# The even layer of a two-layer encoder with its tokens in parity order, and its first two value products side by side

## The chip, the core and the metric

The kernel runs on one core of a Trainium2 chip. The core has five engines that run at the same time, each with its own queue that is worked off in order: TensorE (PE) multiplies matrices, VectorE (DVE) and ScalarE (ACT) work element by element, GpSimd (POOL) and SyncE (SP) mostly start DMA transfers here. The engines wait for each other through semaphores. The metric is the device time of one execution in microseconds; 2482.04 us is the median of three runs before the change.

## The reference

The input is x with 256 tokens of 2048 numbers. Layer 0 is an even layer, layer 1 an odd one; each is a mixer with a residual, then a gated feed-forward network with a residual. What the change touches is the mixer of layer 0:

```python
y = rmsnorm(h, ln_mix[layer])
proj = einsum("bsd,de->bse", y, w_in)
# A: eight heads, three groups (window, dilation) = (128, 1), (512, 4), (2048, 16)
logits = q . k * scale + t5_bias(offset); p = softmax; o = p @ v     # per group, lse kept
out_a  = sum over groups of softmax(lse) * o
# B: four heads, two maps each
w = softmax(q1 . k1 + bias) - lam * softmax(q2 . k2 + bias);  o = rmsnorm(w @ v)
mix = concat(out_a, out_b) @ w_out
```

Groups 1 and 2 of A have dilations 4 and 16, so a query sees only keys whose distance is even. The bias of a pair depends on the bucket of key position minus query position.

## The kernel before, in words

All of the work is built around products of a 2048 by N weight with the activations of 256 tokens. Both sides are kept as two numbers in float32r, a high part and the remainder, and a product is three matmuls: high by high, high by low, low by high. Every weight unit of 512 KB is fetched by SP into `raw` (5 buffers), rounded by ACT into `wh` (L196) and subtracted by DVE into `wl` (L197). `wh` and `wl` have 4 buffers each. So the cast of unit n writes over unit n-4 and waits until PE has read that one for the last time.

There are two kinds of product. `gemm_b` (L129, L132) has weights as the stationary operand and gives queries and keys. `gemm_a` (L157 to L159) has the activations stationary and the weights moving, 512 columns at a time, and gives the values V and the output projections: 8 units, 12 matmuls each, 96 per product. Its result takes two PSUM buffers of the tag `gm`, of which there are four.

The even layer needs six V products in A, three per half of the heads (groups 0, 1, 2). Those of groups 1 and 2 need the tokens with the even ones first; `strided` reads every other column of the stationary activations (L154). The layer's norm is put in late: the products run on x times the gain (`yT`, from a transposed copy `xT`), and the factor per token `rstd` multiplies the result when V leaves PSUM (`v_tiles`, ACT L200 and DVE L203). `rstd` comes from eight squares of x on ACT (L226, two for each quarter of x), a sum (L245), a square root on ACT (L210, behind a load of its table) and a reciprocal (L212). `row_broadcast` lays it along the columns: two copies (L253), two PE transposes (L254), a copy into R (L256). Two more transposes (L403) and a copy (L404) give `rstd_par`, the factor in parity order.

At the start nine matmuls on zeros run on PE (L371). Then comes the product of group 0, whose units are taken in turn with pieces of `xT`, then two small matmuls in float32 that make the tables of biases (L410, L415), then the product of group 1, then `v_tiles` of group 0 and the rest. The tables go by DMA from POOL to DRAM (`rel`, `rel2`) and come back per head in a skewed form. The tile `vals`, from which `rel` is written, and the scratch of the squares share one buffer of the tag `junk`.

The order in which an engine's instructions stand is set by a scheduler that works on the written program; instructions that are marked (`keep_in_program_order`) stay where they are. Functions given to `later` are called some products later by `tick`.

Of the kernel before, what the change touches and what calls it, by code (L numbers as in the profile page):

```python
# [25 lines left out]
F32 = mybir.dt.float32  # L27
# [5 lines left out]
P = 128  # L33
SEQ = 256
# [23 lines left out]
def trunk_kernel(ctx: ExitStack, tc, a, out):  # L58
# [46 lines left out]
    def wunit(src, parts=1):  # L105
# [36 lines left out]
    def a_unit(ps, src, u, act, nk, strided=False, parts=1):  # L142
        last = 2 * u + 2 == nk
        a_products(ps, wunit(src[u], parts), u, act, nk, strided,
                   [(t, k) for t in range(2) for k in range(2)] if last else
                   [(t, k) for k in range(2) for t in range(2)])

    def a_products(ps, w, u, act, nk, strided, order):
# [12 lines left out]
    def gemm_a(src, act, nk, strided=False, hooks={}, first=1):  # L161

        ps = [tps("gm", 4), tps("gm", 4)]
        for u in range(nk // 2):
            if u in hooks:
                hooks[u]()
            a_unit(ps, src, u, act, nk, strided, parts=1 if u else first)
# [15 lines left out]
    def halves(ps, r, order=None):  # L183
# [11 lines left out]
    def split(dst_h, dst_l, src):  # L195
        S.copy(dst_h, src)  # L196
# [51 lines left out]
    def row_broadcast(rstd):  # L248
# [7 lines left out]
        V.tensor_copy(r, ps[:, 0:SEQ])  # L256
# [63 lines left out]

    def bias_view(b, step):
# [52 lines left out]
    def x_half(u):  # L374

        xt = att.tile([P, 2, SEQ], F32, name=nm("xT"), tag=f"qk{2 + u % 4}", bufs=1)
        nc.sync.dma_start(xt.rearrange("p a b -> p (a b)"), a["xT"][u])
        for k in range(2):
            yT.append(y_tile(xt[:, k, :], ln[:, 0, :], u * 2 + k, pin=True))

    def x_rows(c):
# [5 lines left out]
    v_ps = [gemm_a(a["eva_v"][0], yT, KT, hooks={u: lambda u=u: x_half(u) for u in range(8)}, first=2)]  # L387
    table = load("t5", (32, 28), eng=nc.sync)
    onehot = load("onehot", (32, NREL), pool=tmp, tag="rx", eng=nc.sync)
    bmask = load("bmask", (28, NREL), pool=tmp, tag="ry", eng=nc.sync)  # L390
    onehot2 = load("onehot2", (32, 256), pool=tmp, tag="rx", eng=nc.sync)
    bmask2 = load("bmask2", (16, 256), pool=tmp, tag="ry", eng=nc.sync)
# [9 lines left out]
    for t in range(2):  # L402
        T.transpose(ps[:, t, 0:P], R.rearrange("p (j r) -> p r j", r=2)[:, t, :], ident)  # L403
    V.tensor_copy(rstd_par, ps[:, :, 0])  # L404

    rel = dram.tile([28, NREL + 1], F32, name="rel")
    rel2 = dram.tile([16, 256], F32, name="rel2")
    vals = tmp.tile([28, NREL + 1], F32, name="vals", tag="junk", bufs=1)
    ps = tps("s", 2)
    T.matmul(ps[0:28, 0:NREL], table, onehot, start=True, stop=True)  # L410
    V.tensor_tensor(vals[:, 0:NREL], ps[0:28, 0:NREL], bmask, op=ALU.add)
    G.dma_start(rel[:, 0:NREL], vals[:, 0:NREL])
    vals2 = tmp.tile([16, 256], F32, name="vals2", tag="rb")
    ps = tps("s", 2)
# [516 lines left out]
```

## Time and profile before

| | us |
|---|---|
| median of three runs | 2482.04 |
| the profiled execution's own time | 2482.04 |
| its span, first to last instruction | 2480.2 |
| PE busy in the span | 2469.6 |
| DVE busy | 1656.3 |
| ACT busy | 1242.2 |

The share of busy time of PE is one of a pipeline: a matmul of 512 columns is shown as 0.39 us long, but the next one starts 0.227 us after it. What one costs is read from the starts that follow each other. Times in the trace count from the start of the span; the execution's own time is 1.8 us longer than the span.

### The profile page before, as it was taken

The page shows a single profiled execution, that of the slowest core. Times are in us where ns is not written, and L with a number is a line of the kernel's source. Part 1 is how long each engine was busy: PE and PEld are TensorE (multiplying, and loading weights), DVE is VectorE, ACT ScalarE, POOL GpSimd, SP SyncE. Part 2 cuts the span into 40 slices and gives each one's busy share as a digit, 9 for nine tenths or more (in the row PEclk, how much of TensorE's full clock was granted, in tenths as well). Part 3 has the DMA queues.
Part 4 walks back from the last instruction along what each step waited for, and adds up shares of the span by engine and source line. Part 5 has one row for each costly group of instructions (what it writes and reads, how often), then busy time and mean ns, then how long its engine had stood idle before and what let it go on. Part 6 is the DMA issues. An engine that isn't in the chain of part 4 may idle for free.

```text
span 2480.2 us, 34338 instructions
## 1 busy us (share of the span) xinstructions
PE 2469.6 (100%) x13115; PEld 2125.7 (86%) x13115; DVE 1656.3 (67%) x2460; ACT 1242.2 (50%) x1859; POOL 44.2 (2%) x71
## 2 busy tenths in 40 slices
PE   9999999999999999999999999999999999999998
PEld 7888888888888888888888888888888888888887
DVE  6676567676577775477775568665777755777754
ACT  6454445465554444344444457545544443444543
POOL 0000000000000000000000000100000000000000
PEclk9999999999999999999999999999999999999999
DMA  8655566556555665566665555765566655666664
GB/s 290 194 174 178 180 182 187 173 180 180 174 187 187 188 190 195 193 188 190 191 189 193 187 184 165 174 176 178 185 190 188 192 191 194 189 192 188 188 195 144
DMA packets 130239, 463.86 MB, mean 187 GB/s; under 512 B 15248, under 2 KB 15884, under 8 KB 130074
## 3 DMA queue, kind: packets, MB, share of 16 engines
q1 hardware_dynamic: 127018, 455.05, 57.2%
q0 software_dynamic: 2624, 6.32, 2.7%
q8 instruction: 102, 1.67, 0.3%
q14 instruction: 63, 0.52, 0.1%
q10 hardware_dynamic: 432, 0.30, 0.0%
HBM read 459.44 MB, written 2.17 MB: 186 GB/s over the span
## 4 chain that ended last, share of the span: by engine, by line
PE 99%; DMA 0%; DVE 0%; ACT 0%; SPq 0%; issue 0%; DVEq 0%
PE gm L129 38%; PE gm L132 20%; PE gm L158 13%; PE gm L157 13%; PE gm L159 13%; PE tp L333 0%; PE tp L240 0%; PE s L317 0%; PE s L318 0%; PE s L316 0%; DMA raw<-in_eva_v 0%; PE s L477 0%; PE s L446 0%; PE s L345 0%; PE s L344 0%; PE s L470 0%
## 5 line engine op out<-in xcount | busy, mean ns | idle before, releaser
L197 DVE TENSOR_TENSOR wl<-raw,wh 128x1024 fp32r<-128x1024 f32 (+1 forms) x857 | 1046.4, 1222 | 414.3 <-ACT wh L196 411.1
L196 ACT CAST wh<-raw 128x1024 fp32r<-128x1024 f32 (+1 forms) x857 | 899.8, 1050 | 549.9 <-PE gm L159 422.2
L129 PE MATMUL gm<-yT,wh 128*128 128x512 f32 x4096 | 991.2, 391 | 0.0
L129 PEld LDWEIGHTS gm<-yT,wh 128*128 128x128 f32 x4096 | 748.9, 188 | 142.7
L132 PEld LDWEIGHTS gm<-yT,wl 128*128 128x128 f32 x4096 | 525.9, 191 | 21.6 <-ACT yT L200 1.2
L132 PE MATMUL gm<-yT,wl 128*128 128x256 f32 x4096 | 534.0, 283 | 0.0
L187 DVE TENSOR_TENSOR t<-t,gm 128x256 f32<-128x256 f32 x256 | 107.6, 420 | 333.7 <-ACT t L186 333.7
L186 ACT COPY t<-gm 128x256 f32<-128x256 f32 x256 | 95.4, 372 | 389.9 <-PE gm L129 389.7
L157 PE MATMUL gm<-wh,prod 128*128 128x512 f32 x704 | 274.4, 390 | 0.0
L159 PE MATMUL gm<-wh,prod 128*128 128x512 f32 x704 | 274.2, 390 | 0.0
L158 PE MATMUL gm<-wl,prod 128*128 128x512 f32 x704 | 273.9, 389 | 0.0
L158 PE MATMUL gm<-wl,yT 128*128 128x512 f32 x416 | 163.7, 394 | 0.5 <-DVE wl L197 0.5
L157 PE MATMUL gm<-wh,yT 128*128 128x512 f32 x416 | 163.9, 396 | 0.3 <-ACT wh L196 0.3
L159 PE MATMUL gm<-wh,yT 128*128 128x512 f32 x416 | 163.2, 392 | 0.0
L158 PEld LDWEIGHTS gm<-wl,prod 128*128 128x128 f32 x704 | 132.2, 188 | 27.4
L157 PEld LDWEIGHTS gm<-wh,prod 128*128 128x128 f32 x704 | 132.2, 188 | 27.2
L159 PEld LDWEIGHTS gm<-wh,prod 128*128 128x128 f32 x704 | 132.2, 188 | 27.2
L623 ACT ACTIVATE cv<-cv 128x256 f32<-128x256 f32 x88 | 36.8, 419 | 166.0 <-DVE cv L621 166.0
L157 PE MATMUL gm<-wh,mix 128*128 128x512 f32 x256 | 101.0, 395 | 0.0
L158 PE MATMUL gm<-wl,mix 128*128 128x512 f32 x256 | 100.4, 392 | 0.0
L159 PE MATMUL gm<-wh,mix 128*128 128x512 f32 x256 | 100.2, 393 | 0.0
L158 PEld LDWEIGHTS gm<-wl,yT 128*128 128x128 f32 x416 | 79.3, 191 | 17.1 <-DVE wl L197 1.4
(215 smaller groups left out, 1548.9 us busy)
## 6 DMA issues: line engine op xcount, KB each, us to landing
raw<-in_up SPq DMA_DIRECT2D x352, 512.0 KB, 3.6
raw<-in_down SPq DMA_DIRECT2D x176, 512.0 KB, 3.7
raw<-in_eva_qk SPq DMA_DIRECT2D x96, 512.0 KB, 3.4
raw<-in_eva_v SPq DMA_DIRECT2D x47, 512.0 KB, 4.0
raw<-in_evb_qk SPq DMA_DIRECT2D x32, 512.0 KB, 3.4
raw<-in_ev_out SPq DMA_DIRECT2D x32, 512.0 KB, 3.4
raw<-in_od_qk SPq DMA_DIRECT2D x32, 512.0 KB, 3.8
raw<-in_od_out SPq DMA_DIRECT2D x32, 512.0 KB, 3.4
```

What stands on the lines that cost most here:

```text
L129: T.matmul(flat, wh[:, sl], y.rearrange("p a b -> p (a b)"), start=(u == 0 and k == 0), stop=(u * 8 + k == KT - 1))
L132: T.matmul(ps[:, 1, :], wl[:, sl], y[:, 0, :], start=False, stop=False)
L157: T.matmul(ps[t], ah, wh[:, sl], start=(kt == 0), stop=False)
L158: T.matmul(ps[t], ah, wl[:, sl], start=False, stop=False)
L159: T.matmul(ps[t], al, wh[:, sl], start=False, stop=(kt == nk - 1))
L186: S.copy(t0, ps[:, 0, :])
L187: V.tensor_tensor(t0, t0, ps[:, 1, :], op=ALU.add)
L196: S.copy(dst_h, src)
L197: V.tensor_tensor(dst_l, src, dst_h.bitcast(F32), op=ALU.subtract)
L623: S.activation(c, c, AF.Gelu_apprx_tanh)
```

## The change

The transposed copy of x, from which the layer's activations are made, holds the even tokens first and then the odd ones. So all of the even layer's products have their tokens in that order, no stationary operand is read with a stride, and the reorderings that stood at single places go or move: `halves` needs no parity order, R is made in parity order, the bias is read in parity order (`parity_bias`, `by_parity`), and B's result is put back in order at its end.

The first two V products (groups 0 and 1) run side by side: for each of eight steps one piece of `xT`, one unit of the first and one of the second. All four `gm` buffers are taken by them. Their `v_tiles` all use `rstd_par`. The first unit's two halves are cast with the second activation tile in between, in a fixed order.

The tables of biases are made inside this loop, after the sixth step, by two float32r matmuls from a high and a low part of the table (`rel_tables`); the table of the even strides is every other column of the one result.

```diff
-    def wunit(src, parts=1):
+    def wunit(src, parts=1, between=None):
...
-            split(wh[:, sl], wl[:, sl], raw[:, sl])
+            split(wh[:, sl], wl[:, sl], raw[:, sl], pin=between is not None)
+            if between and i == 0:
+                between()
...
-            if strided:
-                ah, al = (act[kt][:, x, :].rearrange("p (j r) -> p r j", r=2)[:, t, :] for x in range(2))
-            else:
-                ah, al = (act[kt][:, x, t * P:(t + 1) * P] for x in range(2))
+            ah, al = (act[kt][:, x, t * P:(t + 1) * P] for x in range(2))
...
-        if order in (parity, parity_rev):
-            V.tensor_tensor(order(t2), natural(t0), natural(r), op=ALU.mult)
-        else:
-            V.tensor_tensor(order(t2) if order else t2, t0, r, op=ALU.mult)
+        V.tensor_tensor(order(t2) if order else t2, t0, r, op=ALU.mult)
...
-        V.tensor_copy(r, ps[:, 0:SEQ])
+        if by_parity:
+            V.tensor_copy(parity(r), natural(ps[:, 0:SEQ]))
+        else:
+            V.tensor_copy(r, ps[:, 0:SEQ])
...
-    v_ps = [gemm_a(a["eva_v"][0], yT, KT, hooks={u: lambda u=u: x_half(u) for u in range(8)}, first=2)]
...
-    v_ps.append(gemm_a(a["eva_v"][1], yT, KT, strided=True,
-                       hooks={u: lambda u=u: x_rows(u) for u in range(4)}))
...
+        th, tl = (tmp.tile([32, 28], F32R, name=nm("t5"), tag=f"t5{x}", bufs=1) for x in range(2))
+        split(th, tl, table)
+        oh = tmp.tile([32, NREL + 1], F32R, name="onehot_r", tag="scc")
+        S.copy(oh, onehot)
+        ps = tps("s", 2)
+        T.matmul(ps[0:28, :], th, oh, start=True, stop=False)
+        T.matmul(ps[0:28, :], tl, oh, start=False, stop=True)
+        vals = tmp.tile([28, NREL + 1], F32, name="vals", tag="junk", bufs=1)
+        V.tensor_tensor(vals, ps[0:28, :], bmask, op=ALU.add)
+        G.dma_start(rel, vals)
...
+    v_ps = [[tps("gm", 4), tps("gm", 4)] for _ in range(2)]
+    for u in range(8):
+        xt = att.tile([P, 2, SEQ], F32, name=nm("xT"), tag=f"qk{2 + u % 4}", bufs=1)
+        nc.sync.dma_start(xt.rearrange("p a b -> p (a b)"), a["xT"][u])
+        x_tile(xt, u, 0)
+        if u:
+            x_tile(xt, u, 1)
+        for g in range(2):
+            a_unit(v_ps[g], a["eva_v"][g], u, yT, KT, parts=1 if u else 2,
+                   between=None if u or g else lambda: x_tile(xt, 0, 1))
+        if u == 2:
+            rel_loads()
+        if 3 <= u < 7:
+            x_rows(u - 3)
+        if u == 5:
+            rel_tables()
+        tick()
     for c in range(4):
         squares(c)
-    rstd = row_factor()
-    R = row_broadcast(rstd)
+    R = row_broadcast(row_factor(), by_parity=True)
...
-            vg.append(v_tiles(ps, rstd_par if g else rstd, range(8 + 4 * g, 12 + 4 * g)))
+            vg.append(v_tiles(ps, rstd_par, range(8 + 4 * g, 12 + 4 * g)))
```

What this does to the order on ACT: the eight squares (`junk`, from x in `h`) and the casts of weight units (`wh`). Before, they stood in pairs among the casts of group 1's product, with the square root's table behind the last pair:

```order
L226 ACTIVATE junk_83_480,ssq_78_471<-h_75 128x512
L226 ACTIVATE junk_84_482,ssq_78_471<-h_75 128x512
L196 CAST wh_61_364<-raw_60_362 128x1024
L226 ACTIVATE junk_85_484,ssq_78_471<-h_75 128x512
L226 ACTIVATE junk_86_486,ssq_78_471<-h_75 128x512
L196 CAST wh_64_383<-raw_63_381 128x1024
L210 ACT_TABLE_LOAD
L210 ACTIVATE var_88_490<-var_88_490 128x2
```

In the changed kernel this stands at the same place; `wh_76` and `wh_79` are the last units of the two side-by-side products, `wh_110` to `wh_119` the first four units of the third one:

```order
L194 CAST wh_79_473<-raw_78_471 128x1024
L226 ACTIVATE junk_83_492,ssq_81_489<-h_75 128x512
L194 CAST wh_110_549<-raw_109_547 128x1024
L226 ACTIVATE junk_84_494,ssq_81_489<-h_75 128x512
L194 CAST wh_113_567<-raw_112_565 128x1024
L226 ACTIVATE junk_85_496,ssq_81_489<-h_75 128x512
L194 CAST wh_116_585<-raw_115_583 128x1024
L226 ACTIVATE junk_86_498,ssq_81_489<-h_75 128x512
L194 CAST wh_119_603<-raw_118_601 128x1024
L226 ACTIVATE junk_87_500,ssq_81_489<-h_75 128x512
L226 ACTIVATE junk_88_502,ssq_81_489<-h_75 128x512
L226 ACTIVATE junk_89_504,ssq_81_489<-h_75 128x512
```

The squares moved behind the casts: the first (`junk_82`) stands just ahead of `wh_79`, and the last three behind `wh_119`, which takes the buffer of `wh_79`. Behind `junk_89` follow the table load, the root and the four `v_tiles` of ACT.

On PE, the end of the product ahead of the third one, before (`tp` are the transposes of `row_broadcast` and of `rstd_par`, `gm_106` and `gm_107` the third product):

```order
L157 MATMUL gm_53_322<-wh_76_455,yT_48_290 128x512
L158 MATMUL gm_53_322<-wl_77_456,yT_48_290 128x512
L159 MATMUL gm_53_322<-wh_76_455,yT_48_290 128x512
L254 MATMUL tp_90_495<-ident_93,rb_91_496 128x128
L254 MATMUL tp_90_495<-ident_93,rb_92_499 128x128
L157 MATMUL gm_106_539<-wh_109_543,yT_5_102 128x512
L158 MATMUL gm_106_539<-wl_110_544,yT_5_102 128x512
L159 MATMUL gm_106_539<-wh_109_543,yT_5_102 128x512
L157 MATMUL gm_107_540<-wh_109_543,yT_5_102 128x512
L403 MATMUL tp_95_507<-ident_93,R_93_502 128x128 x2
```

And the same place in the changed kernel, where the third product writes `gm_107` and `gm_108`:

```order
L158 MATMUL gm_5_103<-wh_79_473,yT_74_450 128x512
L159 MATMUL gm_5_103<-wl_80_474,yT_74_450 128x512
L160 MATMUL gm_5_103<-wh_79_473,yT_74_450 128x512
L254 MATMUL tp_93_513<-ident_93,rb_94_514 128x128
L254 MATMUL tp_93_513<-ident_93,rb_95_517 128x128
L443 MATMUL tp_98_525<-ident_93,R_96_520 128x128 x2
L158 MATMUL gm_107_545<-wh_110_549,yT_7_106 128x512
```

The four transposes now stand together ahead of the third product, and that product's first matmul writes the buffer of `gm_2`, which `v_tiles` has to empty first.

## Rows read from the trace of the kernel before

**Rows 1.** The page: busy time, share of the span and count of PE and others; and the chain of work that ended last, as shares of the span by engine.

```profile
PE 2469.6 (100%) x13115; PEld 2125.7 (86%) x13115; DVE 1656.3 (67%) x2460; ACT 1242.2 (50%) x1859; POOL 44.2 (2%) x71
...
PE 99%; DMA 0%; DVE 0%; ACT 0%; SPq 0%; issue 0%; DVEq 0%
```

**Rows 2.** The timeline of PE in the first 13 us: start, length (both us), engine, line, what it writes and reads, how many in one row, and in brackets the idle time before it and who ended that.

```profile
1.49 4.21 PE L371 MATMUL s<-zeros 128*128 128x512 f32 x9 [1.49 <-DVE zeros L368]
5.49 1.06 PE L157 MATMUL gm<-wh,yT 128*128 128x512 f32 x2
...
6.71 0.40 PE L159 MATMUL gm<-wh,yT 128*128 128x512 f32 x1
...
8.63 0.39 PE L159 MATMUL gm<-wh,yT 128*128 128x512 f32 x1
9.33 0.73 PE L157 MATMUL gm<-wh,yT 128*128 128x512 f32 x2 [0.31 <-ACT wh L196]
10.59 0.50 PE L158 MATMUL gm<-wl,yT 128*128 128x512 f32 x1 [0.53 <-DVE wl L197]
```

**Rows 3.** The timeline of PE from the first product (group 0, activations read in one piece) over the two tables into the second (group 1, read with a stride). Between the first two rows' starts, 20.29 and 29.13, lie 39 matmuls, and as many between the last two's, 42.32 and 51.51.

```profile
20.29 0.39 PE L159 MATMUL gm<-wh,yT 128*128 128x512 f32 x1
...
29.13 0.39 PE L159 MATMUL gm<-wh,yT 128*128 128x512 f32 x1
29.45 1.04 PE L410 MATMUL s<-onehot,t 32*28 32x511 f32 x2
...
31.08 0.60 PE L415 MATMUL s<-onehot,t 32*16 32x256 f32 x2
31.61 0.51 PE L158 MATMUL gm<-wl,yT 128*128 128x512 f32 x1
...
42.32 0.40 PE L159 MATMUL gm<-wh,yT 128*128 128x512 f32 x1
...
51.51 0.40 PE L159 MATMUL gm<-wh,yT 128*128 128x512 f32 x1
```

**Rows 4.** The timeline of PE in the second half's product of group 1, read with a stride: between the two starts lie 51 matmuls.

```profile
257.77 0.39 PE L159 MATMUL gm<-wh,yT 128*128 128x512 f32 x1
...
269.67 0.39 PE L159 MATMUL gm<-wh,yT 128*128 128x512 f32 x1
```

**Rows 5.** The timeline of PE where the second product ends and the third begins, and where the third ends and the first product of queries begins.

```profile
53.87 0.38 PE L254 MATMUL tp<-ident,rb 128*128 128x128 f32 x2
54.00 0.48 PE L157 MATMUL gm<-wh,yT 128*128 128x512 f32 x1
...
55.02 0.46 PE L403 MATMUL tp<-ident,R 128*128 128x128 f32 x2
...
76.99 1.32 PE L129 MATMUL gm<-yT,wh 128*128 128x512 f32 x5
```

**Rows 6.** The timeline of ACT from 31 to 40 us: squares, casts, the table load, the root, a cast that follows a root, `v_tiles`, and a cast that waits for PE.

```profile
31.80 0.63 ACT L226 ACTIVATE junk<-h 128x512 f32<-128x512 f32 x1 [0.25 <-DMA h<-in_x]
...
32.56 0.63 ACT L226 ACTIVATE junk<-h 128x512 f32<-128x512 f32 x1
33.10 0.19 ACT L226 ACTIVATION_READ_ACCUMULATOR junk<-h 128x1 f32 x1
33.19 1.04 ACT L196 CAST wh<-raw 128x1024 fp32r<-128x1024 f32 x1
34.24 1.28 ACT L210 ACT_TABLE_LOAD   x1
35.54 0.20 ACT L210 ACTIVATE var<-var 128x2 f32<-128x2 f32 x1
35.65 1.04 ACT L196 CAST wh<-raw 128x1024 fp32r<-128x1024 f32 x1
36.59 1.26 ACT L200 ACTIVATE v<-gm,rstd 128x512 fp32r<-128x512 f32 x2
...
39.93 1.05 ACT L196 CAST wh<-raw 128x1024 fp32r<-128x1024 f32 x1 [1.15 <-PE gm L159]
```

**Rows 7.** The timeline of DVE: the table's values, then the steps from the root to the factor per token, and `v_tiles`.

```profile
33.40 0.67 DVE L411 TENSOR_TENSOR vals<-s,bmask 28x511 f32<-28x511 f32 x1
...
35.78 0.17 DVE L212 RECIPROCAL rstd<-var 128x2 f32<-128x2 f32 x1 [0.29 <-ACT var L210]
35.98 0.36 DVE L253 COPY rb<-rstd 128x128 f32<-128x128 f32 x2
...
54.52 0.40 DVE L256 COPY R<-tp 128x256 f32<-128x256 f32 x1
...
56.30 0.15 DVE L404 COPY rstd_par<-tp 128x2 f32<-128x2 f32 x1
57.21 1.41 DVE L203 SCALAR_TENSOR_TENSOR v<-gm,rstd_par,v 128x512 fp32r<-128x512 f32 x2 [0.76 <-ACT v L200]
```

**Rows 8.** The timeline of POOL: the first load of a bias, which waits until the table has been written to DRAM.

```profile
38.53 1.13 POOL L430 DMA_DIRECT2D bias<-rel  x2 [3.47 <-DMA rel<-vals]
```

**Rows 9.** Stretches of 1 us at the end of the span: the stretch, its length, busy time and count of each engine, the granted clock of PE as a share of 2.4 GHz, the DMA engines' share, GB/s.

```profile
2474.00:2475.00 1.00, 0.00 (x0) 0.00 (x0) 0.97 (x3) 0.97 (x2) 0.00 (x0) 0.73 0.00 0
2475.00:2476.00 1.00, 0.00 (x0) 0.00 (x0) 0.17 (x1) 0.15 (x1) 0.00 (x0) 0.50 0.63 233
```

**Rows 10.** The last matmul of the program in the timeline of PE.

```profile
2471.54 0.39 PE L159 MATMUL gm<-wh,prod 128*128 128x512 f32 x1
```

More of the change, by code (lines that the diff above doesn't have):

```diff
@@ L159, in a_products, with gemm_a @@
             T.matmul(ps[t], al, wh[:, sl], start=False, stop=(kt == nk - 1))
-    def gemm_a(src, act, nk, strided=False, hooks={}, first=1):
+    def gemm_a(src, act, nk, hooks={}):
         ps = [tps("gm", 4), tps("gm", 4)]
@@ L166, in gemm_a @@
                 hooks[u]()
-            a_unit(ps, src, u, act, nk, strided, parts=1 if u else first)
+            a_unit(ps, src, u, act, nk)
             if u % 2 == 1:
@@ L372, in trunk_kernel, with x_tile @@
     yT = []
[L374 to L379, printed above, removed]
+    def x_tile(xt, u, k):
+        yT.append(y_tile(xt[:, k, :], ln[:, 0, :], u * 2 + k, pin=True))
     def x_rows(c):
@@ L386, in trunk_kernel @@
     make_identity(nc, ident)
-    v_ps = [gemm_a(a["eva_v"][0], yT, KT, hooks={u: lambda u=u: x_half(u) for u in range(8)}, first=2)]
[L388 to L392, printed above, removed]
-    v_ps.append(gemm_a(a["eva_v"][1], yT, KT, strided=True,
-                       hooks={u: lambda u=u: x_rows(u) for u in range(4)}))
+    rel = dram.tile([28, NREL + 1], F32, name="rel")
@@ new lines, in trunk_kernel, with rel_loads, rel_tables @@
+    rel2 = dram.tile([28, 256], F32, name="rel2")
+    rel_in = []
+    def rel_loads():
+        for name, width, tag in (("t5", 28, "rb"), ("onehot", NREL + 1, "rx"), ("bmask", NREL + 1, "ry"),
+                                 ("bmask2", 256, "ry")):
+            rel_in.append(load(name, (28 if "bmask" in name else 32, width), pool=tmp, tag=tag, eng=nc.sync))
+    def rel_tables():
+        table, onehot, bmask, bmask2 = rel_in
+        th, tl = (tmp.tile([32, 28], F32R, name=nm("t5"), tag=f"t5{x}", bufs=1) for x in range(2))
[8 more added lines that the diff above has]
+        G.dma_start(rel, vals)
+        vals2 = tmp.tile([28, 256], F32, name="vals2", tag="t0")
+        V.tensor_tensor(vals2, ps[0:28, :].rearrange("p (j r) -> p r j", r=2)[:, 1, :], bmask2, op=ALU.add)
+        G.dma_start(rel2, vals2)
@@ L402, in trunk_kernel, with row_bias @@
     for t in range(2):
-        T.transpose(ps[:, t, 0:P], R.rearrange("p (j r) -> p r j", r=2)[:, t, :], ident)
+        T.transpose(ps[:, t, 0:P], R[:, t * P:(t + 1) * P], ident)
     V.tensor_copy(rstd_par, ps[:, :, 0])
[L406 to L414, printed above, removed]
-    T.matmul(ps[0:16, 0:256], table[:, 8:24], onehot2, start=True, stop=True)
-    V.tensor_tensor(vals2, ps[0:16, 0:256], bmask2, op=ALU.add)
-    G.dma_start(rel2, vals2)
     def new_sc():
         return att.tile([P, 2, 512], F32, name=nm("sc"), tag="sc", bufs=1)
+    def row_bias(row):
+        b = att.tile([P, 384], F32, name=nm("bias"), tag="bias", bufs=2)
+        G.dma_start(b[:, 0:257], bass.AP(tensor=rel.tensor, offset=rel.offset + row * (NREL + 1),
+                                         ap=[[2, P], [1, 257]]))
+        return b
     def a_bias(hd, g):
@@ L579, in b_finish @@
             y = new_act("mix", 8 + 2 * hd + f)
-            split_scaled(y[:, 0, :], y[:, 1, :], ps[:, f, :], sub_gain[:, f:f + 1])
+            split_scaled(natural(y[:, 0, :]), natural(y[:, 1, :]), parity_rev(ps[:, f, :]), sub_gain[:, f:f + 1])
             mix[8 + 2 * hd + f] = y
     for pair in range(2):
-        vt = v_tiles(gemm_a(a["evb_v"][pair], yT, KT), rstd, range(20 - 4 * pair, 24 - 4 * pair))
+        vt = v_tiles(gemm_a(a["evb_v"][pair], yT, KT), rstd_par, range(20 - 4 * pair, 24 - 4 * pair))
         for hd in (2 * pair, 2 * pair + 1):
-            bias = att.tile([P, 384], F32, name=nm("bias"), tag="bias", bufs=2)
-            G.dma_start(bias, bass.AP(tensor=rel.tensor, offset=rel.offset + (24 + hd) * (NREL + 1),
-                                      ap=[[1, P], [1, 384]]))
+            bias = row_bias(24 + hd)
             sc = []
@@ L839, in _constants @@
 def _constants():
-    rel = np.arange(NREL) - (SEQ - 1)
+    rel = np.arange(NREL + 1) - (SEQ - 1)
     onehot = (_t5_bucket(rel)[None, :] == np.arange(32)[:, None]).astype(np.float32)
-    bmask = np.zeros((28, NREL), np.float32)
+    bmask = np.zeros((28, NREL + 1), np.float32)
     bmask[:8] = np.where(np.abs(rel) <= 64, 0.0, NEG)[None, :]
-    d2 = 2 * (np.arange(256) - 127)
-    onehot2 = (_t5_bucket(d2)[None, :] == np.arange(32)[:, None]).astype(np.float32)
-    bmask2 = np.concatenate([np.repeat(np.where(d2 % dil == 0, 0.0, NEG)[None, :], 8, axis=0)
-                             for dil in (4, 16)]).astype(np.float32)
+    d2 = rel[1::2]
+    bmask2 = np.zeros((28, 256), np.float32)
+    for g, dil in ((1, 4), (2, 16)):
+        bmask2[g * 8:g * 8 + 8] = np.where(d2 % dil == 0, 0.0, NEG)[None, :]
     t = np.arange(SEQ)
```

45 lines of the change are left out of this document (25 added, 20 removed).

## The prediction

> **What bounds the kernel now.** I read the page first. PE is busy all the time, and the chain that ended last is PE for 99% [rows 1]. So a step counts only if it changes what PE does or when PE may go on; work that moves on DVE, ACT or POOL counts where PE comes to wait for it. Then I read PE's timeline where the change stands, the first 77 us, by the starts that follow each other. Three things are to be seen. In the first product PE has holes: nothing starts between 8.63 and 9.33, and two matmuls begin between 9.33 and 10.59, both times with ACT or DVE named as what was waited for [rows 2]. The two tables stand in the way for about 2 us [rows 3]. And the products that read their activations with a stride run at a slower step than the first one [rows 3, 4]. PE goes from the second product into the third nearly without a hole, from 53.87 to 54.00 [rows 5], because the squares, the root and the factor were done on ACT and DVE 18 us earlier [rows 6, 7]. Behind 77 us the instructions of all engines stand in the same order in both kernels, the four second-half strides aside, so I leave that part as it is.
>
> The sum is made against the profiled execution's own 2482.04 us, which is also the median of the three runs.
>
> **Strides (gain 3.0).** Read in one piece, a matmul takes (29.13 - 20.29)/39 = 0.2267 us; with a stride (51.51 - 42.32)/39 = 0.2356 us [rows 3]. That is 0.0090 x 96 = 0.86 us for the product of group 1, and I take the same for group 2 of that half. In the second half it is (269.67 - 257.77)/51 = 0.2333 [rows 4], so 0.0067 x 192 = 1.28. Together 3.0 us.
>
> The Trainium skill ("SBUF — State Buffer", on the port swizzle) says that float32 data may be read with a stride of up to four elements for free, as two accesses to one 16-byte line hide the step. By it the stride of two here costs nothing and this term would be 0. The rows show 7 to 9 ns per matmul, and I go by them.
>
> **Start (gain 1.4).** From 5.49 to the end of the first product's last step, 29.13 + 0.23 = 29.36, pass 23.87 us [rows 2, 3]; 96 steps of 0.2267 are 21.76. Of the 2.11 us over, three matmuls from 5.49 to 6.71 take 1.22 instead of 0.68 because the clock is still low: 0.54, which stays. Left are 1.57, of which 0.47 lie between 8.63 and 9.33 and 0.81 between 9.33 and 10.59 [rows 2]. These were waits for the second unit. Side by side, each piece of x brings two units, 5.4 us of PE, the second unit comes in halves, and ACT has two casts of 0.94 and two activations to do in that time. I take 1.4 off; the bounds are 0 (the second unit comes as late as before) and 1.6.
>
> **Tables (gain 1.2).** From 29.36 to 31.61 pass 2.25 us, with two product matmuls of 0.23 in them, so the tables cost 1.80 [rows 3]. The new pair is float32r with 512 columns: two steps of 0.23 and some 0.1 for the change of shape, 0.6. No row shows a matmul of 32 rows in float32r, so the bounds are 0.4 (steps alone) and 1.0 (as the first old pair took, 29.45 to about 30.4). Gain 1.2, between 0.8 and 1.4.
>
> **The wait ahead of the third product (cost 9.7).** Here something new comes in. The first two products now hold all four PSUM buffers, and they end together. The third may start only when `v_tiles` has emptied the first buffer, which needs `rstd_par`, which needs the last square. The second product ended at 53.87 [rows 5]; with 1.4, 0.86 and 1.2 taken off, both end at 50.4, and the last matmul's result is there at 50.6.
>
> When does the last square end? In the new order the last three stand behind the cast `wh_119`, and that cast may not start before PE has read `wh_79`, the last unit of the two products, for the last time. The trace shows this rule of four buffers: a cast starts at 39.93, when a product matmul has ended [rows 6]. That alone puts the cast at 50.6. But ACT is late already. The first square writes the buffer of `vals` and must wait until `rel` has been written to DRAM. The new tables stand ahead of unit 13 of 16, four units of 2.72 us before 50.4, so at 39.5; 0.17 for the result and 0.67 for the values on DVE [rows 7] make 40.3. In the trace, POOL goes on 4.46 us after the values are done (33.40 + 0.67 = 34.07, then 38.53) [rows 7, 8]. So the first square starts at 44.8. Behind it squares and casts alternate: 0.63 from a square to a cast (32.56 to 33.19), 0.94 from a cast to the next (35.65 to 36.59) [rows 6], 1.57 a pair. `wh_119` starts at 44.8 + 4 x 1.57 + 0.63 = 51.7, the three squares follow at 52.65, 53.4 and 54.2 (0.76 each, 31.80 to 32.56), and the last ends 0.73 later, at 54.9. PE's own units come through: `wl` of its last unit is ready at about 47.7, when it is wanted.
>
> The Trainium skill ("DMA: Bandwidth & Descriptors", on the anatomy of a DMA by GpSimd) gives about 2.0 us fixed for such a transfer. By it the first square would start near 42.5 and the cast would wait for PE alone; the wait would be 1.1 us shorter. The trace has 4.46 for the same transfer, and that is used.
>
> From 54.9 nothing lies beside other work: the table load to the root's start 1.30 (34.24 to 35.54) and on to the reciprocal 0.24, 0.20 to the copies, 0.36 for them [rows 6, 7]: 57.0. Two transposes 0.38 and the copy into R 0.40 [rows 5, 7], two more transposes 0.46 [rows 5], the copy 0.15, one `v_tiles` on ACT 0.65 (1.26 for two) and one on DVE 0.70 (1.41 for two) [rows 6, 7]: 2.74, and about 0.06 for each of six handovers: 60.1. From 50.4 to 60.1 are 9.7 us. Bounds: 8.6, if only PE's release counts, and 10.7, if the copy into R in parity order or the table's write takes longer. Off go the old transposes: 53.87 to 76.99 are 23.12, and 96 x 0.2356 are 22.62, so 0.5 [rows 3, 5].
>
> **The clock (cost 2.2).** At the end of the program the last matmul ends at 2471.93 [rows 10]; in the stretch from 2474 the mean granted clock is 0.73, behind it 0.50 [rows 9]. So it fell from 2.4 to 1.2 GHz at about 2474.46, after 2.5 us without a matmul. The new hole is over 6 us up to the first transposes. At the program's start nine matmuls of zeros take 0.444 each, and the step is down to 0.23 only from 6.71 on, after 12 matmuls [rows 2]. So the third product should begin at the low level and do some 11 matmuls at 0.2 us more each: 2.2, between 0 (the clock stays, or the transposes bring it back) and 2.6.
>
> DVE loses 40 reorderings, POOL's loads get shorter: off the path, nothing.
>
> **Sum.** Gains 3.0 + 1.4 + 1.2 + 0.5 = 6.1. Costs 9.7 + 2.2 = 11.9. Net +5.8: 2482.04 + 5.8 = 2487.8 us.
>
> **Rivals.**
> - *The hole stays hidden (faster).* The squares are done in the V products' shadow as before, so the third product starts at once: 2482.04 - 6.1 + 0.5 = 2476.4. It is so if the casts between the squares don't wait, and decides where the last square ends before about 45. For it speaks that x is in SBUF long before; against it the cast at 39.93, which did wait for PE [rows 6]. Chance 0.05.
> - *The clock does not count.* It stays up or comes back with the transposes: 2487.8 - 2.2 = 2485.6. Rows 9 speak against it, but they show the end of a program. Chance 0.2.
> - *The table's write is quick*, and ACT is not late: 2487.8 - 1.1 = 2486.7. Chance 0.15.
> - *The stride was not the cause* of the slower step: +3.0, 2490.8. For it: the second half's step is less slow than the first's though the stride is the same [rows 3, 4]. Against: both are slower than plain ones. Chance 0.05.
> - *Side by side PE waits* for casts or transfers, as ACT and SP now carry the same start with more behind it: the start's gain is lost, 2489.2. Chance 0.1.
>
> **How the numbers follow.** The forecast keeps 0.45. The low end is the highest gains with the shortest wait and no clock: -6.5 + 8.6 = +2.1, 2484.1. The high end is the lowest gains (2.7 + 0.5 + 0.8 + 0.5 = 4.5) with a wait of 10.7 and 2.2 for the clock: +8.4, 2490.4. The range 2484.0 to 2490.4 leaves out little but the faster rival and a part of the tails. What a measurement of this kernel can tell is about 0.2%, 4.96 us: faster is below 2477.1, slower above 2487.0. Faster has the first rival, 0.05. Above 2487.0 lie seven tenths of the forecast, most of the last two rivals and a part of the third: 0.55. The rest, 0.40, is no change.
>
> **What would show it.** On PE, starts 0.227 us apart in all six V products; the second unit starting before 9.0; a hole of about 6 us from 50.6 on, ended by the transposes of L254, and the first matmul of the third product near 60 with DVE's `v` as what it waited for. On ACT, the first square waiting for the table's DMA until near 44.8, and three squares behind the cast of 51.7. The granted clock at 0.5 for some microseconds after the hole. The first queries' product near 84 instead of 76.99. It is wrong if the third product starts less than 5 us after the second, or if the clock stays at 1.0.

## The result and the profile after

The changed kernel takes 2487.79 us (median of 13 runs, 2486.85 to 2488.38) against 2481.79 us for the kernel before (13 runs, 2481.28 to 2482.06): ratio 1.0023, 95% interval 1.0016 to 1.0031. It is slower by 6.0 us; the forecast was 5.8. The profiled execution took 2488.19 us, its span is 2486.4.

On the page the two profiles can hardly be told apart. This is the page of the changed kernel, its busy times and the chain that ended last, as in [rows 1].

```profile
PE 2468.5 (99%) x13113; PEld 2125.2 (85%) x13113; DVE 1654.4 (67%) x2462; ACT 1244.7 (50%) x1862; POOL 44.0 (2%) x71
PE 99%; DMA 0%; ACT 0%; DVE 0%; issue 0%; DVEq 0%; ACTq 0%
```

The loss is a hole of some 9.6 us in 2486, and only the list of PE's waits and its timeline show it. All waits of PE in the changed kernel (who waited, for whom, us in total, times, longest):

```profile
PE tp L254 <- DVE rb L253: 5.7, 1, 5.7
PE gm L158 <- DVE v L203: 1.8, 1, 1.8
PE s L381 <- DVE zeros L378: 1.5, 1, 1.5
PE tp L443 <- DVE R L257: 0.7, 1, 0.7
```

The third line is in both kernels (zeros at the program's start); the other three are new. PE's timeline of the changed kernel, at the start, at the tables, from the last V product to the third product, and at the first product of queries; it answers to [rows 2, 3, 5]:

```profile
8.28 0.39 PE L158 MATMUL gm<-wh,yT 128*128 128x512 f32 x1
...
11.45 0.39 PE L160 MATMUL gm<-wh,yT 128*128 128x512 f32 x1
...
38.73 0.39 PE L160 MATMUL gm<-wh,yT 128*128 128x512 f32 x1
39.05 0.41 PE L410 MATMUL s<-onehot_r,t 32*28 32x512 f32 x1
39.31 0.38 PE L411 MATMUL s<-onehot_r,t 32*28 32x512 f32 x1
39.62 0.50 PE L158 MATMUL gm<-wh,yT 128*128 128x512 f32 x1
...
50.41 0.39 PE L160 MATMUL gm<-wh,yT 128*128 128x512 f32 x1
56.47 0.66 PE L254 MATMUL tp<-ident,rb 128*128 128x128 f32 x2 [5.68 <-DVE rb L253]
57.82 0.69 PE L443 MATMUL tp<-ident,R 128*128 128x128 f32 x2 [0.69 <-DVE R L257]
60.27 0.80 PE L158 MATMUL gm<-wh,yT 128*128 128x512 f32 x1 [1.76 <-DVE v L203]
...
84.43 1.75 PE L133 MATMUL gm<-yT,wh 128*128 128x512 f32 x7
```

The holes of the old start are gone: from 8.28 to 11.45 the 14 steps take 3.17 us, 0.226 each. The matmul ahead of the tables starts at 38.73 and has its step of 0.23, so the tables cost 39.62 - 38.96 = 0.66. The last matmul of the two V products starts at 50.41; with one step of 0.23 they end at 50.64 (the bracket at 56.47 counts to the end of that matmul's record, 56.47 - 5.68 = 50.79). From there to 60.27 PE does four transposes and nothing else. ACT's timeline of the changed kernel tells why the transposes are late; it answers to [rows 6]:

```profile
42.78 0.63 ACT L226 ACTIVATE junk<-h 128x512 f32<-128x512 f32 x1 [4.93 <-DMA rel<-vals]
...
51.17 1.04 ACT L194 CAST wh<-raw 128x1024 fp32r<-128x1024 f32 x1 [1.39 <-DMA raw<-in_eva_v]
...
54.16 0.19 ACT L226 ACTIVATION_READ_ACCUMULATOR junk<-h 128x1 f32 x1
54.37 1.28 ACT L210 ACT_TABLE_LOAD   x1
...
58.74 2.42 ACT L200 ACTIVATE v<-gm,rstd_par 128x512 fp32r<-128x512 f32 x4 [2.88 <-DVE rstd_par L444]
```

The first square waits 4.93 us for the write of `rel`; the last three stand behind a cast that waits for its weight. DVE's timeline of the changed kernel, against [rows 7]:

```profile
39.73 0.68 DVE L413 TENSOR_TENSOR vals<-s,bmask 28x512 f32<-28x512 f32 x1 [5.24 <-PE s L411]
...
57.17 0.60 DVE L257 COPY R<-tp 128x256 f32<-128x256 f32 x1 [0.70 <-PE tp L254]
```

And PE's granted clock (the column behind the count) in the hole and behind it:

```profile
54.00:56.00 2.00, 0.00 (x0) 0.71 1.02 365
...
64.00:65.00 1.00, 1.00 (x4) 0.50 0.00 0
65.00:66.00 1.00, 1.00 (x5) 0.96 0.00 0
```

A mean of 0.71 over 54 to 56 is 0.84 us at 1.00 and the rest at 0.50: the clock fell from 2.4 to 1.2 GHz at 54.8, 4 us after the last product matmul. From 64 to 65 it is still 0.50, from 65 to 66 the mean is 0.96: it was back near 65.1.

### The profile page after: what moved, and what is told of

Same layout as the page of the kernel before. It is cut to its first block, busy times and chain, and to the rows that moved or that the text cites. A ratio compares the mean times of both kernels' runs of the same rounds, so it can differ in the third digit from the quotient of the medians.

```text
span 2486.4 us, 34339 instructions
## 1 busy us (share of the span) xinstructions
PE 2468.5 (99%) x13113; PEld 2125.2 (85%) x13113; DVE 1654.4 (67%) x2462; ACT 1244.7 (50%) x1862; POOL 44.0 (2%) x71
## 4 chain that ended last, share of the span: by engine, by line
PE 99%; DMA 0%; ACT 0%; DVE 0%; issue 0%; DVEq 0%; ACTq 0%
PE gm L133 38%; PE gm L136 20%; PE gm L158 13%; PE gm L159 12%; PE gm L160 12%; PE tp L343 0%; PE tp L240 0%; PE s L320 0%; PE s L319 0%; PE s L321 0%; DMA raw<-in_eva_v 0%; PE s L507 0%; PE s L476 0%; PE s L381 0%; PE s L355 0%; PE s L500 0%
## 5 line engine op out<-in xcount | busy, mean ns | idle before, releaser
L190 DVE TENSOR_TENSOR t<-t,R 128x256 f32<-128x256 f32 x216 | 91.7, 424 | 6.6
```

## The experiments

Where the trace of a run is compared, one number is handy: the start of the first product of queries, behind which nothing differs but the strided products of the second half. It is 76.99 before and 84.43 after.

**1. The squares, the root and the factor taken into the loop.**

```diff
-        vals = tmp.tile([28, NREL + 1], F32, name="vals", tag="junk", bufs=1)
+        vals = tmp.tile([28, NREL + 1], F32, name="vals", tag="scc")
...
+            if u == 7 and g == 0:
+                for t in range(2):
+                    T.transpose(ps[:, t, 0:P], R[:, t * P:(t + 1) * P], ident)
+                V.tensor_copy(rstd_par, ps[:, :, 0])
...
+        if 3 <= u < 7:
+            squares(u - 3, pin=True)
+        if u == 6:
+            R = row_broadcast(row_factor(), by_parity=True)
...
-    for c in range(4):
-        squares(c)
-    R = row_broadcast(row_factor(), by_parity=True)
```

> The changed kernel with its side by side products kept, but the squares of a token's row, the root, R and the two transposes for the factor by parity taken into the loop (squares at steps 3 to 6, pinned; R after step 6; the factor between the two units of step 7), and the table's values in a buffer that no square needs. Theory (the cost is the wait ahead of the third product, 9.5 us from the last V product's end to 60.27, and the low clock behind it, 2.2): no result is waited for but the eviction of the first two banks, which are full 2.7 us before the end; the third product starts at 51 to 52, at 1.00, and the time falls by 10 to 11 us, to about 2477, 0.998 of the kernel before. Rival 1 (the wait is hidden, something later is late anyway): 2485 to 2488. Rival 2 (the low clock costs nothing of its own): 2479. Rival 3 (the blocked VectorE at 34.5 to 39.7 us and the late weights of unit 19 cost as much when they stand alone): the last V products wait and the gain is under 8 us.

Measured: 2476.69 us, ratio 0.9979 (0.9971 to 0.9988), 11.1 less than the changed kernel and 5.1 less than the kernel before. It beats both. In PE's timeline of this run the factor's transposes have a product matmul right behind them, no wait is shown, and the queries begin at 73.25:

```profile
48.52 0.38 PE L433 MATMUL tp<-ident,R 128*128 128x128 f32 x2
48.66 0.47 PE L158 MATMUL gm<-wh,yT 128*128 128x512 f32 x1
...
73.25 1.98 PE L133 MATMUL gm<-yT,wh 128*128 128x512 f32 x8
```

84.43 - 73.25 = 11.2: the whole difference lies ahead of the queries. PE waits for nothing in the first 100 us but the zeros. DVE still stands 5.13 us at the table's values in this run (its timeline, below), and PE comes to wait for nothing by it: rival 3 falls.

```profile
40.09 0.68 DVE L415 TENSOR_TENSOR vals<-s,bmask 28x512 f32<-28x512 f32 x1 [5.13 <-PE s L413]
```

This run changes three things at once: the buffer, the place of the squares and the place of the factor. Experiments 2, 7 and 8 take them apart.

**2. Only the buffer of the table's values.**

```diff
-        vals = tmp.tile([28, NREL + 1], F32, name="vals", tag="junk", bufs=1)
+        vals = tmp.tile([28, NREL + 1], F32, name="vals", tag="scc")
```

> The changed kernel with one word changed: the table's values get a buffer of their own instead of the one that the squares write. The scheduler then puts the squares beside the later steps of the loop and the root ahead of the last step. Theory (over half of the wait ahead of the third product is the row of squares behind the transfer of the table): R's transposes follow the last V product at once, as in the run with the products in sequence, where 4.1 us lie from R's transposes (52.36) to the third product (56.49) and 7 matmuls ran at 1.2 GHz; so the third product starts at 54.6 to 55 instead of 60.27 and 4 of 11 slow matmuls (0.8) go: 6.3 us less than the changed kernel, about 2481.5. Rival (the squares are late because of the weight of unit 19, which lands at 51.1, and not because of the transfer): under 1 us less, 2487 to 2488. Rival 2 (the clock falls all the same for 11 matmuls): 2482.3.

Measured: 2483.38 us, ratio 1.0005 (0.9996 to 1.0014): 4.4 of the 6.3. One word changes the order that the scheduler makes on ACT: in this run's timeline of ACT the squares are over and the table load begins at 37.29, where the changed kernel had not begun its first.

```profile
35.74 0.63 ACT L226 ACTIVATE junk<-h 128x512 f32<-128x512 f32 x1
...
37.29 1.28 ACT L210 ACT_TABLE_LOAD   x1
...
51.09 1.04 ACT L194 CAST wh<-raw 128x1024 fp32r<-128x1024 f32 x1 [2.18 <-DMA raw<-in_eva_v]
```

PE's timeline of the same run has what is left:

```profile
50.38 0.38 PE L254 MATMUL tp<-ident,rb 128*128 128x128 f32 x2
51.46 0.44 PE L443 MATMUL tp<-ident,R 128*128 128x128 f32 x2 [0.70 <-DVE R L257]
55.22 0.80 PE L158 MATMUL gm<-wh,yT 128*128 128x512 f32 x1 [3.33 <-DVE v L203]
...
60.51 0.62 PE L158 MATMUL gm<-wh,yT 128*128 128x512 f32 x1
```

R's transposes no longer wait; the third product starts 5.05 us earlier. But 13 matmuls, not 7, run at the low clock, 0.4 us more than the 11 of the changed kernel, and the weight that lands at 51.09 delays the factor's copy on DVE: `wl` of that weight runs from 52.16, and the copy into `rstd_par` stands behind it, at 53.51. 5.05 - 0.4 = 4.65, and 4.4 are measured. So about half of the wait (5.05 of 9.6) was the squares' place behind the table's write; the rest is the factor, which comes out of R's transposes when both products are done, with the late weight in its way.

**3. Work for PE in the hole, read by nobody.**

```diff
+    def fill(n):
+        ps = tps("s", 2)
+        y = yT[0]
+        for _ in range(n):
+            tc.keep_in_program_order(T.matmul(ps, y[:, 0, 0:P], y.rearrange("p a b -> p (a b)"), start=True, stop=True))
...
+    fill(24)
     R = row_broadcast(row_factor(), by_parity=True)
...
     V.tensor_copy(rstd_par, ps[:, :, 0])
+    fill(6)
```

> The changed kernel with 24 matmuls 128x512 between the last V product and R's transposes, and 6 behind the transposes for the factor by parity; their sums are read by nobody. 24 x 0.227 = 5.4 us, so they end about 56.2, ahead of the row that R's transposes wait for (56.47). Theory (of the 11.9 us between the two kernels' third products 2.2 are the 11 matmuls at 1.2 GHz): the third product starts at about 60.3 as before the edit, all its matmuls at 1.00, the time falls by 2.0 to 2.4 us to 2485.4 to 2485.8. Rival (the low clock is made up for later, or the fall has another cause than the idle TensorE): 2487.5 to 2488.0, with the same 11 matmuls at 0.427 us or with none of them and no gain.

Measured: 2485.19 us, ratio 1.0014 (1.0005 to 1.0023), 2.6 less than the changed kernel with 30 matmuls more. The clock stays at 1.00, and the third product goes at full pace from its second row on (PE's timeline of this run):

```profile
50.35 5.60 PE L423 MATMUL s<-yT 128*128 128x512 f32 x24
55.86 0.41 PE L254 MATMUL tp<-ident,rb 128*128 128x128 f32 x2
...
59.17 0.50 PE L158 MATMUL gm<-wh,yT 128*128 128x512 f32 x1 [0.38 <-DVE v L203]
59.50 0.40 PE L159 MATMUL gm<-wl,yT 128*128 128x512 f32 x1
```

The third product also starts 1.1 us earlier. Half of that is the clock too: the two pairs of transposes take 0.41 and 0.44 here, 0.66 and 0.69 in the changed kernel. The other 0.6 is the cast of the late weight (50.55 instead of 51.17), which is no part of the edit. The low clock's price is therefore read from the traces and not from the 2.6: from the third product's first start to the queries pass 84.43 - 60.27 = 24.16 us in the changed kernel and 81.08 - 59.17 = 21.91 here, so the slow matmuls of the third product cost 2.25 us, and the slow transposes 0.5 more.

**4. The same with the products of experiment 2**, and 14 matmuls behind the factor's transposes.

> The version with the values' own buffer (2483.4), and 14 matmuls 128x512 behind the transposes for the factor by parity, whose sums nobody reads; they end about 55.2, where the third product started. In the run of that version 13 matmuls from 55.22 to 60.51 were 0.43 instead of 0.23 us apart, 2.6 us in all. Theory (term Clock): none of them is slow, 2480.8, and the third product starts no later than 55.4. Rival (the low clock's cost is made good elsewhere): 2483.4. Rival 2 (the added matmuls put the third product back by what they take beyond the wait): up to 1 us of the gain is lost.

Measured: 2481.09 us, ratio 0.9996 (0.9987 to 1.0005), 2.3 less than experiment 2. The third product starts at 55.41, behind the 14 matmuls (0.2 later than in experiment 2), and the granted clock is 1.00 in every stretch from 52 to 60. From the third product's start to the queries pass 24.58 us in experiment 2 and 21.89 here, so its 13 slow matmuls cost 2.7 us by the traces. So twice the low clock has the price of its slow matmuls.

**5. The old stride, dropped from the kernel before.**

```diff
-            if strided:
-                ah, al = (act[kt][:, x, :].rearrange("p (j r) -> p r j", r=2)[:, t, :] for x in range(2))
-            else:
+            if True:
                 ah, al = (act[kt][:, x, t * P:(t + 1) * P] for x in range(2))
```

> The kernel before with one thing changed: the V products of groups 1 and 2 read their stationary token columns side by side, not every other one; this leaves out that their tokens come even ones first. All else, in order and number, is as before. Theory (term Strides: 192 matmuls at 0.2356 instead of 0.2267 in the first half and 192 at 0.2333 instead of 0.2267 in the second): 3.0 us less, 2478.8, 0.9988 of before; the strided matmuls of the second half fall from 0.2333 to about 0.227 us. Rival (the pitch comes from the stage, from DMA or PSUM, and not from the stride; the Trainium skill, SBUF -- State Buffer, states that a stride of up to 4 free elements costs nothing): 0, 2481.8, the pitch as before.

Measured: 2479.20 us, ratio 0.9989 (0.998 to 0.9998): 2.6 less, against 3.0 by the term. The step falls as expected: in the second half 150 matmuls lie between the starts 254.04 and 288.04 of this run's timeline of PE, 34.00/150 = 0.2267 us. The order is as before, and so are the waits but one, PE's for `wh` at the start (0.8 us and not 0.3), which lies ahead of the strided products. Where the last of them ends and queries begin the traces are 2.7 us apart (291.67 and 294.40). So the stride alone makes the slower step.

**6. Steps of 3 and 4 instead of 2.**

```diff
-                ah, al = (act[kt][:, x, :].rearrange("p (j r) -> p r j", r=2)[:, t, :] for x in range(2))
+                y = act[kt]
+                ah, al = (bass.AP(tensor=y.tensor, offset=y.offset + t + x, ap=[list(y.ap[0]), [strided, P]])
+                          for x in range(2))
...
-            ps = v_ps.pop(0) if v_ps else gemm_a(a["eva_v"][hh * 3 + g], yT, KT, strided=(g > 0))
+            ps = v_ps.pop(0) if v_ps else gemm_a(a["eva_v"][hh * 3 + g], yT, KT, strided=(0, 4, 3)[g])
```

> The kernel before, with its strided stationary reads at a step of 4 elements in group 1 and of 3 in group 2 instead of 2 in both; the 128 columns then run over the high and the low part, so the V values of these groups are not those of the reference. Measures the pitch in the second half, where 96 matmuls of each group stand one behind the other: 0.227 plain and 0.2333 at a step of 2 are known. Theory (the cost is of reading the stationary operand and grows with the step): 0.235 to 0.25 at 3 and 0.24 to 0.27 at 4, 384 matmuls, 1 to 10 us more than before. Rival (any step but 1 costs the same): 0.2333 for both, 2481.8. Rival 2 (as the Trainium skill's SBUF -- State Buffer has it, a step up to 4 is free and something else made 0.2333): as before, 2481.8, and no difference between the groups.

Measured: 2482.96 us, ratio 1.0005 (0.9996 to 1.0014), 1.1 more than before. PE's timeline of this run in the second half, group 1 (step 4; 77 steps between the first two rows) and group 2 (step 3; 84 between the last two):

```profile
254.00 0.40 PE L161 MATMUL gm<-wh,yT 128*128 128x512 f32 x1
...
272.10 0.39 PE L160 MATMUL gm<-wl,yT 128*128 128x512 f32 x1
...
275.15 0.40 PE L161 MATMUL gm<-wh,yT 128*128 128x512 f32 x1
...
294.94 0.40 PE L161 MATMUL gm<-wh,yT 128*128 128x512 f32 x1
```

18.10/77 = 0.2351 and 19.79/84 = 0.2356, beside 0.2333 at a step of 2 and 0.227 at 1. In the first half the step of 2 already cost 0.2356 [rows 3]. Nearly the whole price in time between matmuls is paid at 2; it does not grow with the step. That is rival 1, with 2 ns on top in the second half.

The theory is right in one thing that the distance of the matmuls does not show. These are the weight loads of PE (PEld, the reading of the stationary operand) by groups of one line: count, busy time in us, mean length in ns. The first is of experiment 5 (step 1, 252 to 291 us), the second of the kernel before (step 2, 273 to 294), the last two of this run (step 3, 274 to 294, and step 4, 252 to 272):

```profile
L155 PEld LDWEIGHTS gm<-wh,yT 128*128 128x128 f32 x58 | 10.9, 188 | 2.2
L157 PEld LDWEIGHTS gm<-wh,yT 128*128 128x128 f32 x30 | 5.8, 193 | 1.2
L161 PEld LDWEIGHTS gm<-wh,yT 128*128 128x128 f32 x29 | 7.3, 252 | 0.0
L159 PEld LDWEIGHTS gm<-wh,yT 128*128 128x128 f32 x28 | 8.7, 310 | 0.0
```

The load itself grows with the step, from 188 ns to 193, 252 and 310. At 3 and 4 it is longer than the 0.235 us from one matmul to the next, and yet the matmuls come hardly later than at 2.

**7. The first two products one after the other again**, in parity order, with the new tables.

```diff
-        for g in range(2):
-            a_unit(v_ps[g], a["eva_v"][g], u, yT, KT, parts=1 if u else 2,
-                   between=None if u or g else lambda: x_tile(xt, 0, 1))
+        a_unit(v_ps[0], a["eva_v"][0], u, yT, KT, parts=1 if u else 2,
+               between=None if u else lambda: x_tile(xt, 0, 1))
...
+    for u in range(8):
+        if u < 4:
+            x_rows(u)
+        a_unit(v_ps[1], a["eva_v"][1], u, yT, KT)
```

> The changed kernel with its first two V products one after the other again, as in the kernel before (all eight units of the first, then those of the second, squares and R beside the second), and the table's values in a buffer that no square needs; parity order, the tables from H/L parts and the plain reads stay. Theory (all of the loss is the side by side order): no wait ahead of the third product, the strides' 3.0, the tables' 1.2 and 0.5 for the old transposes are gained, the start's 1.4 is not: 4.7 less than before, 2477.1, ratio 0.998. Rival 1 (the parity order costs elsewhere, in the bias sums or the copies that go by parity): 2480 or more. Rival 2 (the start's excess goes by the half casts alone): 2475.7.

Measured: 2483.91 us, ratio 1.0008 (0.9999 to 1.0017). The theory that the side by side order is the whole loss falls: 6.8 us are missing. The timeline of PE shows where:

```profile
52.36 0.38 PE L254 MATMUL tp<-ident,rb 128*128 128x128 f32 x2
53.45 0.44 PE L446 MATMUL tp<-ident,R 128*128 128x128 f32 x2 [0.70 <-DVE R L257]
56.49 0.50 PE L158 MATMUL gm<-wh,yT 128*128 128x512 f32 x1 [2.61 <-DVE v L203]
```

A hole, though the root was done beside the second product. From 52.36 to 56.49 are 4.1 us, and the slow matmuls behind it cost some 1.6 (23.53 us from the third product's start to the queries, 21.94 in experiment 8, where the hole is gone). A part of the rest is the start, where the first product's last matmul begins at 29.57 and not at 29.13 [rows 3]. In the kernel before, `v_tiles` of group 0 takes `rstd`, which DVE has at 35.78 [rows 7], and empties two buffers long before the third product wants them. In parity order group 0 as well takes `rstd_par`, and that comes out of R's transposes, which stand behind all V products on PE. So the new theory: the factor's new way is a second cause, whatever the order of the products.

**8. The same with the factor early.**

```diff
+        if u < 4:
+            squares(u, pin=True)
         if u == 5:
             rel_tables()
+            R = row_broadcast(row_factor(), by_parity=True)
+            Rq = query_factor(R)
+        if u == 6:
+            rstd_par = const.tile([P, 2], F32, name="rstd_par")
...
```

> The run with the products in sequence once more, with the squares at the second product's first four steps, R behind its sixth and the factor by parity behind its seventh, so that no transpose is waited for behind the last V product. Theory (what that run lost against its 2477.1 is the factor by parity, which comes out of R's transposes behind all V products: 3.3 us of waits and 7 slow matmuls, 1.4 to 1.9): 5.3 us less than 2483.9, 2478.6; and above the version with the products side by side and the factor early (2476.7) by the start's 1.5 alone, 2478.2. Rival 1 (the parity order costs in other places): 2480 or more. Rival 2 (side by side gains nothing at the start once the wait is gone): 2476.7.

Measured: 2478.65 us, ratio 0.9987 (0.9978 to 0.9995), 5.3 less than experiment 7, as the new theory has it. The holes of the start are there again (PE's timeline of this run), and with them this version's median stands 2.0 us above experiment 1:

```profile
8.95 0.39 PE L160 MATMUL gm<-wh,yT 128*128 128x512 f32 x1
9.58 0.73 PE L158 MATMUL gm<-wh,yT 128*128 128x512 f32 x2 [0.24 <-ACT wh L194]
10.84 0.51 PE L159 MATMUL gm<-wl,yT 128*128 128x512 f32 x1 [0.53 <-DVE wl L197]
```

By the traces the side by side order is worth 1.6 us by itself: the queries begin at 74.81 here and at 73.25 in experiment 1. Behind the queries the two runs have the same products, so the other 0.4 of the medians is not shown to come from the order.

**9. The tables alone, in the kernel before.**

```diff
+    rel_loads()
+    hooks = {u: lambda u=u: x_rows(u) for u in range(4)}
+    hooks[6] = rel_tables
+    v_ps.append(gemm_a(a["eva_v"][1], yT, KT, strided=True, hooks=hooks))
...
-    T.matmul(ps[0:28, 0:NREL], table, onehot, start=True, stop=True)
...
-    T.matmul(ps[0:16, 0:256], table[:, 8:24], onehot2, start=True, stop=True)
```

> The kernel before with the tables alone as in the changed kernel: one product of two matmuls from the H and L parts, inside the second V product ahead of its seventh unit, and the second table read as every other column of it; the table's values in a buffer that no square needs. The two old table matmuls behind the third product's first ones are gone. Theory (term Tables: 1.80 us of TensorE become 0.6): 1.2 less, 2480.6, ratio 0.9995. Rival (the old ones stood where something else would have been waited for): 0, 2481.8. Rival 2 (VectorE, which stands at the values until the table's matmuls are done, brings the weights late): 2482 or more, with a wait of TensorE for weights in the second product.

Measured: 2480.59 us, ratio 0.9995 (0.9986 to 1.0004), 1.4 less than the before of its runs (2481.98). The scheduler set the two matmuls ahead of the second product, at 29.38, and not ahead of its seventh unit; the term does not depend on that. By itself this difference is smaller than its interval, so the term is read from the trace: the tables take 29.94 - 29.29 = 0.65 us on PE (29.06 is the last start ahead of them, with one step of 0.23) and not 1.80, a gain of 1.15. The queries begin 1.6 us earlier (75.39), because something else changed too: the second product, still read with a step of 2, goes at (51.98 - 33.31)/80 = 0.2334 us and not at 0.2356, and so does the third (0.2332). Why is not shown.

## Why the prediction was right, and where its sizes were off

| term | forecast | found |
|---|---|---|
| Strides | -3.0 | -2.6 (experiment 5) |
| Start | -1.4 | -1.6 by the traces, -2.0 by the medians (8 against 1) |
| Tables | -1.2 | -1.15 by the trace, -1.4 by the medians (9); 0.66 for the pair, 0.6 forecast |
| wait ahead of the third product | +9.7 | 60.27 - 50.64 = 9.6 |
| old transposes | -0.5 | -0.4 (75.47 - 53.12 = 22.35 with them in 5, 81.08 - 59.17 = 21.91 without in 3) |
| Clock, the third product's matmuls | +2.2 | +2.25 (3) |
| whole | +5.8 | +6.0; the rows above add up to 6.1 |

- **The wait** was the right mechanism at the right size, with parts off in both directions; that 9.7 was met within 0.1 is partly luck. The V products ended 0.2 later than forecast, the last square 0.55 earlier, and the way from it to the third product was 0.7 longer. The last square ended at 54.35, not 54.9. What held the cast `wh_119` was not ACT's lateness: the first square started at 42.78, two microseconds before the forecast's 44.8, and from there the cast would have been due at 42.78 + 4 x 1.57 + 0.63 = 49.7. PE's release came at 50.8, and then its own weight was not there until 51.17. From the last square on, 5.92 us passed instead of 5.2: R's copy in parity order took 0.60, not 0.40, and the transposes ran at the low clock (0.28 and 0.23 more), which the sum had not applied to them.
- **The table's write** was the wrong step: 4.46 us, read where the DMA engines were busy. The same distance in the changed kernel, from the values' end (39.73 + 0.68 = 40.41) to the first square at 42.78, is 2.4. POOL in the kernel before and in the changed one (`rel` issued, `bias` free to load):

```profile
34.37 0.69 POOL L412 DMA_DIRECT2D rel<-vals  x1 [33.06 <-DVE var L209]
38.53 1.13 POOL L430 DMA_DIRECT2D bias<-rel  x2 [3.47 <-DMA rel<-vals]
```

```profile
40.71 0.68 POOL L414 DMA_DIRECT2D rel<-vals  x1 [39.40 <-DVE vals L413]
...
42.99 1.12 POOL L452 DMA_DIRECT2D bias<-rel  x2 [1.09 <-DMA rel<-vals]
```

  4.2 us from issue before, about 2.1 in the changed kernel (ACT, which waits for the same write, goes on at 42.78). The DMA engines were 1.03 busy in 34 to 36 before, and 0.00 in 40 to 41 in the changed kernel, since DVE stood 5.24 us at the values and freed no weight buffer: SP fetches a weight at 34.52 and the next at 41.90, when the first `wl` behind the values is done. The other runs say the same. From issue to landing this write takes 2.0 us in the changed kernel and in experiments 1 to 4, where it comes in such a pause, and 3.9 to 4.9 in the kernel before and in experiments 5 to 9. The Trainium skill ("DMA: Bandwidth & Descriptors", on the anatomy of a DMA by GpSimd) gives some 2.0 us fixed: the changed kernel agrees (2.1), the kernel before does not (4.2). The rival *the table's write is quick* was right on the write and wrong on the time, as the late weight took its place.
- **The clock.** The rival that it does not count falls by experiments 3 and 4. That it falls in such a hole was right; at the program's end it fell 2.5 us after the last matmul, here 4 us after the last product matmul. The count of 11 slow matmuls was met exactly, and that is luck too: 13 were slow in experiment 2 and 7 in experiment 7. It was taken from the program's start, where PE's granted clock reads 1.00 in every stretch from 2 to 8 us; that the clock is low there is read from the matmuls' distance alone (0.444 us, against 0.43 behind the hole, where the clock reads 0.50).
- **Strides.** The rival that the stride was not the cause falls by experiment 5. The Trainium skill ("SBUF — State Buffer", on the port swizzle) has a step of up to four float32 for free; here a step of 2 cost 7 to 9 ns per matmul, and steps 3 and 4 cost 8 to 9.
- **The hole stays hidden**, at 2476.4, was priced right for a kernel that was not this one: experiment 1 makes it so and takes 2476.69.
- **What the working did not say**: that group 0 lost its early factor. It was in the sum, since all four buffers were taken to wait for `rstd_par`; but it was put down to the products ending together. Experiments 7 and 8 show that it costs 5.3 us in sequence too.
- **The range.** Its top, 2490.4, takes 0.5 as the least gain of the start and 2.2 for the clock, where the terms' own bounds are 0 and 2.6; with these it would be 2491.3. The result lies far from it.

## What to carry to other kernels

A change that makes each step cheaper can still move the moment at which a shared buffer comes free: ask of every buffer that the next stage needs what its release waits for, and whether that chain can be run while PE still has work. The tag of a small buffer is such a dependency: one word put eight squares behind a DRAM write. And a hole of several microseconds is paid twice where PE goes on at half its clock behind it, as after the holes of 9.6, 4.8 and 4.1 us here.

## What was not expected of the hardware

- The clock did not fall at the same distance from the last work each time. It fell 4 us after the last product matmul in the changed kernel. In experiment 7 it fell at about 57.6, when PE had been at work again since 56.49, after only 4.1 us in which it did four transposes: 57 to 58 has 0.79 and 58 to 59 has 0.50, and it was back at 61. A short hole can thus cost its slow matmuls after it has been left behind.
- A stationary operand read with a step costs nearly the same distance from matmul to matmul at 2, 3 and 4 (0.2333 to 0.2356 us against 0.2267), while its weight load grows from 188 ns to 310. At a step of 2 the load is 193 ns long where the matmuls are 0.2333 apart, and 196 to 198 where they are 0.2356 apart (the kernel before, second and first half). Why the same step costs the one or the other, and why the longer loads at 3 and 4 hold up PE no more, stays open.
- The same write to DRAM took 2.0 us from issue to landing with the DMA engines nearly idle and 3.9 to 4.9 with them busy, in eleven traces.
